# Two transformer blocks on one core: the experts' normalised tokens stored in eight runs of 128 features

## The chip, the cores and the metric

The kernel runs on one core of one Trainium2 chip, in one launch. The metric is the device time of an execution in microseconds; the time of a kernel is the median of its runs.

## What is computed

The program computes two models one after the other on 512 tokens of 1024 features: four layers with convolution, state-space and RWKV mixers, and then two layers (l = 0, 1) of a token mixer and a mixture of experts. The change lies in the mixture of experts alone, of which this is the core (32 experts in four groups of eight, top 2, 512 hidden features; h is the RMS-normalised token, scaled and shifted):

```python
def hierarchical_moe(h, rg_w, rg_b, re_w, re_b, w1, w3, w2):
    xf = h.reshape(N, D)
    g_logits = (xf @ rg_w).astype(jnp.float32) + rg_b
    g_idx = jnp.argmax(g_logits, axis=-1).astype(jnp.int32)
    ...
    top_l, top_i = lax.top_k(e_logits, TOP_K)
    e_w = jax.nn.softmax(top_l, axis=-1) * g_w
    expert_id = (g_idx[:, None] * EXPERTS_PER_GROUP + top_i).reshape(-1).astype(jnp.int32)
    ...
    def run_block(args):
        toks, wts, e = args
        xb = x_pad[toks]
        hb = jax.nn.silu(xb @ w1[e]) * (xb @ w3[e])
        return (hb @ w2[e]) * wts[:, None].astype(xb.dtype)
```

In the layer it stands as `x = x + g2 * hierarchical_moe(rms_norm(x, norm2_g[l]) * (1 + sc2) + sh2, ...)`.

## The kernel before

The residual is held with features on the partitions, as eight tiles `xp[m]` of 128 features by 512 tokens in fp32. `moe(l)` runs once for each of the two layers.

**Normalised tokens.** The loop at L2475 transposes the residual on TensorE (L2479): for each of four blocks j of 128 tokens and each half q of the features, four transposes fill a PSUM tile with 128 tokens by 512 features. ACT multiplies it by the token's 1/rms and writes `hH`, rounded to fp32r, TensorE's format for fp32 operands (L2481). The rest that the rounding leaves is `hL`, so that two fp32r products give an fp32 one: for q = 1 DVE makes it from PSUM (L2483), for q = 0 ACT writes an unrounded copy `xr` (L2486) and POOL subtracts (L2487). Both are tiles of 128 tokens by 4 blocks by 1024 features, in the order of the features. DVE and POOL work at the same time on the routing (`route`), which gives each token its place among its experts' rows.

**Gathers.** `moe_gather` fetches the tokens of a group of places. A group is a run of experts in the order of work; there are seven in a layer, of N = 192, 288, 320, 320, 256, 320 and 64 places. POOL and DVE build a 0/1 selection matrix `R` (L2443, L2444), and TensorE multiplies: each of eight parts j takes 8 matmuls (4 token blocks of hH, then 4 of hL) into one PSUM tile, with 128 features as the stationary operand and `R`, N columns wide, moving. The expert weights lie so that partition p holds the features 8p to 8p+7, so part j needs the features j, j+8, j+16, ...; the stationary operand is `[:, i % 4, j::8]`, one float in eight (L2453). ACT or DVE scale and shift the part into `xg` (L2457, L2455). PSUM tiles of tag "st" have two buffers.

**Experts.** For each expert six tiles `raw` of 1 MB hold its weights (two halves each of w1, w3, w2), loaded on SP's queue (L2383) into 11 buffers. A load is issued when the buffer's last user on TensorE is done. `moe_up` multiplies the gathered tokens with w1 and w3 (L2400), with the tokens stationary and the weights moving; `moe_down` transposes the gated product (L2419) and multiplies with w2 (L2427); `moe_store` copies the result to a block of rows (L2634), and each full block of 128 rows is multiplied by its selection (L2582, L2583) and added to the residual by DVE (L2558).

**Order.** All engines work in the order in which the program issues. The first group is gathered ahead of the first expert, the following ones in pieces: after each expert's `moe_up` the call `self.fill(fill, 5 if g < 1 else 3)` issues some steps of the next group's gather, so that it is ready when its first expert begins. `last_selections` uses the storage of hH and hL again, after the last gather, for the last two blocks' rows. The loop in `overflow` ran no iteration.

Other lines that the rows below name: L423 is the dense layers' matmul, whose stationary operand is 128 adjacent fp32r weights in each partition; L458 is a column sum, a matmul with 128 adjacent fp32 floats as the stationary operand and one moving column. In the first model, L855 is an ACT copy out of PSUM that reads in steps of eight and writes eight runs of 64; L925 is an ACT function of a PSUM tile read in order; L926 is a DVE product that reads an SBUF and a PSUM operand in steps of eight; L994 is a DVE operation that reads PSUM in steps of 64.

Of the kernel before, what the change touches and what calls it, by code (L numbers as in the profile page):

```python
# [8 lines left out]
FT = mybir.dt.float32  # L9
FR = mybir.dt.float32r  # L10
I32 = mybir.dt.int32
AF = mybir.ActivationFunctionType
OP = mybir.AluOpType
# [4 lines left out]
S = 512  # L18
D = 1024
# [1502 lines left out]
class K2(K):  # L1522
# [908 lines left out]
    def moe_gather(self, l, place, base, n, out, N=320, bufs=2):  # L2431

        nc = self.nc
        V, G, T, ACT = nc.vector, nc.gpsimd, nc.tensor, nc.scalar
        s, X = self.tl(f"sh{N}", (2, 4)), f"{N}" if N < 320 else ""
        if isinstance(base, int):
            (V if base else G).tensor_scalar(s, place, float(-base), None, op0=OP.add)
        else:
            V.tensor_scalar(s, place, base, None, op0=OP.subtract)
        R = self.tl("R" + X, (4, N), FR, bufs)  # L2440
        for j in range(4):
            a = self.tl("Ra" + X, (N if X else S,), bufs=bufs)
            G.tensor_scalar(a[:, :n], self.cm("slot")[:, 0:n], s[:, 0, j:j + 1], None, op0=OP.is_equal)  # L2443
            V.scalar_tensor_tensor(R[:, j, :n], self.cm("slot")[:, 0:n], s[:, 1, j:j + 1], a[:, :n],  # L2444
                                   op0=OP.is_equal, op1=OP.add)
        yield
        x = self.tl("xg" + X, (8, N), bufs=bufs)
        out.append(x)
        gain, shift = self.gp[:, l, 0], self.gp[:, l, 1]
        for j in range(8):  # L2450
            p = self.pt("st", bufs=2)
            for i in range(8):
                T.matmul(p[:, :n], (self.hH, self.hL)[i // 4][:, i % 4, j::8], R[:, i % 4, :n], start=i == 0, stop=i == 7)  # L2453
            if j % 2 and out[1:]:
                V.tensor_scalar(x[:, j, :n], p[:, :n], gain[:, j:j + 1], shift[:, j:j + 1], op0=OP.mult, op1=OP.add)  # L2455
            else:
                ACT.activation(x[:, j, :n], p[:, :n], AF.Identity, scale=gain[:, j:j + 1], bias=shift[:, j:j + 1])  # L2457
            yield

    def moe(self, l, begin):  # L2460
        ro = ExitStack()
        self.ro = ro.enter_context(self.tc.tile_pool(name="ro", bufs=1, reuse_waits="tile"))
        nc, A, mo = self.nc, self.A, self.mo
        V, G, T, ACT = nc.vector, nc.gpsimd, nc.tensor, nc.scalar
        loads = {0: self.moe_loads(l, 0), 1: self.moe_loads(l, 1, self.NRAW - 6)}
        if begin:
            self.moe_before(l)
            for k in range(KT):
                self.moe_part(l, k)
        rstd = self.rms_rows(self.ps2, D)  # L2470
        route = self.route(l, rstd)

        self.hH = mo.tile([128, 4, D], FR, name=f"hH{l}", tag="hH", bufs=1)
        self.hL = mo.tile([128, 4, D], FR, name=f"hL{l}", tag="hL", bufs=1)
        for j in range(4):  # L2475
            for q in range(2):
                p = self.pt()
                for k in range(4):
                    T.transpose(p[:, k * 128:k * 128 + 128], self.xp[q * 4 + k][:, j * 128:j * 128 + 128], self.ident)  # L2479
                h, lo = (a[:, j, q * 512:q * 512 + 512] for a in (self.hH, self.hL))  # L2480
                ACT.activation(h, p, AF.Copy, scale=rstd[:, j:j + 1])  # L2481
                if q:
                    V.scalar_tensor_tensor(lo, p, rstd[:, j:j + 1], h.bitcast(FT), op0=OP.mult, op1=OP.subtract)  # L2483
                else:
                    u = self.ro.tile([128, 512], FT, name=f"xr{l}{j}", tag="xr", bufs=2)
                    ACT.activation(u, p, AF.Copy, scale=rstd[:, j:j + 1])  # L2486
                    G.tensor_tensor(lo, u, h.bitcast(FT), OP.subtract)  # L2487
        main = next(route)
        gx = []
        first = self.moe_gather(l, main, *GROUPS[0], gx)  # L2490
        next(first)
        main = next(route)
        self.fill(first, 99)
        wts, over, eii = next(route)
        ro.close()
        with self.tc.tile_pool(name="ov", bufs=1, reuse_waits="tile") as self.ov:
            self.overflow(l, eii, over, wts)
        self.sc = ro.enter_context(self.tc.tile_pool(name="scat", bufs=1, reuse_waits="tile"))
        self.block = -1, None
        prev, fill, g = None, None, -1  # L2500
        for i, r in enumerate(ORDER):
            if r not in loads:
                e = r if r < NSTATIC else nc.values_load(eii[0:1, r:r + 1], engines=[mybir.EngineType.SP], min_val=0, max_val=31)
                loads[r] = self.moe_loads(l, e)
            ws, rest = loads[r]
            self.fill(rest, 6)
            if g < 0 or PLACE[r] >= sum(GROUPS[g]):
                self.fill(fill, 99)
                g += 1
                fill = self.moe_gather(l, main, *GROUPS[g + 1], gx) if g + 1 < len(GROUPS) else None  # L2510
                if not fill:
                    self.last_selections(l, spread)
            o = PLACE[r] - GROUPS[g][0]
            units = [(o + u, min(CAPS[r] - u, 64)) for u in range(0, CAPS[r], 64)]
            gs = self.moe_up(ws, gx[g], units)
            self.fill(fill, 5 if g < 1 else 3)
            if prev:
                self.moe_store(blocks, *prev)
            else:

                spread = []
                for a in (main[:, 0], main[:, 1], wts[:, 0], wts[:, 1]):
                    p = self.pt("tp", bufs=2)
                    self.spread(p, a)
                    self.uid += 1
                    spread.append(self.sc.tile([128, S], FT, name=f"sp{self.uid}", tag=f"sp{len(spread)}"))
                    last = (V.tensor_copy if len(spread) % 2 else ACT.copy)(spread[-1], p).ins
                if self.lb is None:
                    with self.behind(last):
                        self.lower_bounds()  # L2530
                blocks = [self.moe_block(l, b, spread) for b in range(len(BLOCKS))]
            prev = ws, gs, units, r
        self.moe_store(blocks, *prev)
        self.end_block(blocks)
        ro.close()
# [50 lines left out]

    def last_selections(self, l, spread):

        h, lo = (self.mo.tile([128, 4, D], FR, name=f"{n}{l}e", tag=n, bufs=1) for n in ("hH", "hL"))
        self.ends = []  # L2590
        for i, a in enumerate((h, lo)):
            parts = a.rearrange("p a (b n) -> p (a b) n", n=S)
            w = self.tl("sh320", (2, 4))[:, 0]
            self.ends.append([parts, self.selection(len(BLOCKS) - 2 + i, spread, parts[:, 0], w)])

# [263 lines left out]
```

## Time and profile before

| | |
|---|---|
| time, median of 3 runs | 3482.0 us (3480.37 to 3494.45) |
| the profiled execution's own time | 3500.02 us |
| its span, first to last instruction | 3498.2 us |
| mean granted TensorE clock | 0.902 of full speed |
| PE (matmuls) busy | 3143.2 us, 90%, 23218 instructions |
| PEld (weight loads) busy | 2286.1 us, 65%, 23218 instructions |
| DVE busy | 2005.3 us, 57%, 3911 instructions |
| ACT busy | 1031.4 us, 29%, 1695 instructions |
| POOL busy | 875.1 us, 25%, 738 instructions |

PE is TensorE's matmul stream and PEld its loads of stationary operands, which overlap the matmuls. The granted clock is 1.00 for 2.4 GHz and 0.50 for 1.2 GHz; over a stretch a mean of the two is shown. Busy shares are means over the whole program. The two runs of the expert layer lie at about 1968 to 2590 us and from 2890 us to the end. A wait is put down to the engine and line whose end released it. Matmuls follow each other before the one ahead has ended, so the mean duration of one is longer than the interval between two.

### The profile page before, as it was taken

The numbers are of one execution on the slowest core, as the hardware profiler recorded it, in microseconds if no ns is written. First come the engines' busy times: TensorE is split into PE (matmuls) and PEld (weight loads), VectorE is DVE, ScalarE is ACT, GpSimd is POOL, SyncE is SP. The second block draws the span as 40 slices with busy tenths as digits, with TensorE's granted clock in tenths as the row PEclk, the third lists the DMA queues.
The fourth block names the chain that finished last, engine by engine and source line by source line (L and its number), as shares of the span: only waits on it lengthen the run. The fifth ranks groups of instructions, "written<-read, shape, count | busy, mean of one in ns | idle before, by whom it ended". The sixth has DMA issues, their size and how long they took to land. (4 is left out here: it accounts for less than half of the span.)

```text
span 3498.2 us, 57476 instructions
## 1 busy us (share of the span) xinstructions
PE 3143.2 (90%) x23218; PEld 2286.1 (65%) x23218; DVE 2005.3 (57%) x3911; ACT 1031.4 (29%) x1695; POOL 875.1 (25%) x738
## 2 busy tenths in 40 slices
PE   6999889898878889998699889989979997998998
PEld 5687768765657777786565676556647575665564
DVE  6744584566865776888656444424346744344333
ACT  3233334365433333222343321111125332111111
POOL 2911321234223454412124221001011522010000
PEclk9999899998885888998798889999989887999998
DMA  5453552316676545776310349999952004799997
GB/s 167 129 150 104 154 159 79 103 54 172 185 211 175 174 134 157 204 232 165 82 49 9 127 160 381 382 373 405 387 187 67 19 25 181 302 385 379 416 381 293
DMA packets 443070, 690.46 MB, mean 197 GB/s; under 512 B 68720, under 2 KB 354800, under 8 KB 408944
## 3 DMA queue, kind: packets, MB, share of 16 engines
q1 hardware_dynamic: 441648, 684.63, 57.0%
q8 instruction: 185, 3.03, 0.4%
q10 hardware_dynamic: 1152, 2.10, 0.2%
q14 instruction: 85, 0.70, 0.1%
HBM read 642.08 MB, written 46.94 MB: 197 GB/s over the span
## 5 line engine op out<-in xcount | busy, mean ns | idle before, releaser
L317 DVE TENSOR_TENSOR wl<-wr,wh 128x1024 fp32r<-128x1024 f32 (+2 forms) x275 | 324.6, 1182 | 214.9 <-ACT wh L315 104.8
L315 ACT ACTIVATE wh<-wr 128x1024 fp32r<-128x1024 f32 (+2 forms) x290 | 270.7, 939 | 550.7 <-PE pmm L423 184.9
L2400 PE MATMUL pmm<-raw,xg 128*32 128x128 f32 (+1 forms) x5120 | 357.2, 330 | 0.0
L2400 PEld LDWEIGHTS pmm<-raw,xg 128*32 128x32 f32 (+1 forms) x5120 | 231.9, 125 | 118.8 <-issue 50.0
L2543 POOL TENSOR_SCALAR Ra<-sp,cf 128x512 f32<-128x512 f32 x28 | 44.6, 1593 | 883.2 <-PE pst L2582 820.1
L423 PE MATMUL pmm<-H,wh 128*128 128x512 f32 x680 | 209.5, 418 | 9.6 <-ACT cg L2073 4.0
L423 PE MATMUL pmm<-H,wl 128*128 128x512 f32 x680 | 204.3, 409 | 1.3 <-DVE wl L317 1.3
L423 PE MATMUL pmm<-L,wh 128*128 128x512 f32 x680 | 203.4, 408 | 0.1
L2558 DVE SCALAR_TENSOR_TENSOR xp<-pst,mod,xp 128x512 f32<-128x512 f32 x196 | 142.8, 748 | 69.7 <-PE pst L2583 65.0
L2427 PE MATMUL pas<-raw,gT 128*32 128x256 f32 (+1 forms) x1472 | 167.2, 450 | 12.1 <-DVE gT L2421 9.4
L2453 PE MATMUL pst<-R,hH 128*128 128x320 f32 (+4 forms) x448 | 137.7, 429 | 31.7 <-DVE R L2444 29.3
L423 PEld LDWEIGHTS pmm<-H,wh 128*128 128x128 f32 x680 | 131.9, 199 | 42.6 <-ACT cg L2073 4.2
L1556 DVE SCALAR_TENSOR_TENSOR war<-wa,cs,war 128x256 f32<-128x256 f32 x252 | 155.9, 634 | 3.8
L423 PEld LDWEIGHTS pmm<-H,wl 128*128 128x128 f32 x680 | 132.2, 197 | 34.4 <-issue 3.6
L2453 PEld LDWEIGHTS pst<-R,hH 128*128 128x128 f32 x448 | 118.7, 334 | 52.8 <-DVE R L2444 33.1
L423 PEld LDWEIGHTS pmm<-L,wh 128*128 128x128 f32 x680 | 131.8, 196 | 31.1 <-issue 1.7
L2453 PE MATMUL pst<-R,hL 128*128 128x320 f32 (+4 forms) x448 | 127.3, 412 | 0.0
L2634 ACT COPY Y<-pas 32x256 f32<-32x256 f32 (+1 forms) x92 | 37.8, 411 | 296.0 <-DVE Y L2634 295.9
L2634 DVE COPY Y<-pas 32x256 f32<-32x256 f32 (+1 forms) x92 | 43.7, 475 | 133.8 <-PE pas L2427 126.2
L2427 PEld LDWEIGHTS pas<-raw,gT 128*32 128x32 f32 (+1 forms) x1472 | 59.7, 119 | 91.8 <-issue 56.6
L2453 PEld LDWEIGHTS pst<-R,hL 128*128 128x128 f32 x448 | 119.0, 338 | 0.4 <-issue 0.4
L2407 DVE TENSOR_TENSOR g<-g,pmm 128x256 f32<-128x256 f32 (+1 forms) x56 | 20.3, 363 | 171.8 <-ACT g L2406 171.4
(869 smaller groups left out, 6796.1 us busy)
## 6 DMA issues: line engine op xcount, KB each, us to landing
raw<-in_w_dram SPq DMA_DIRECT2D x384, 1024.0 KB, 9.8
wa<-in_w_ada_dram SPq DMA_DIRECT2D x48, 1024.0 KB, 6.3
wr<-in_conv_w_in_dram SPq DMA_DIRECT2D x64, 512.0 KB, 4.8
wr<-in_w_in_dram SPq DMA_DIRECT2D x34, 512.0 KB, 4.1
wr<-in_ple_gate_dram SPq DMA_DIRECT2D x16, 1024.0 KB, 5.4
wr<-in_rwkv_w_rkvz_dram SPq DMA_DIRECT2D x16, 1024.0 KB, 5.3
wr<-in_conv_w_out_dram SPq DMA_DIRECT2D x8, 1024.0 KB, 5.2
wr<-in_ssm_w_in_dram SPq DMA_DIRECT2D x8, 1024.0 KB, 6.4
```

The lines of the kernel that those rows point to most:

```text
L315: self.nc.scalar.activation(h, x, AF.Copy)
L317: (eng or self.nc.vector).tensor_tensor(l, x, h.bitcast(FT), OP.subtract)
L423: nc.tensor.matmul(ps[i], ws[i][w][:, perm[k]], x[k], start=n == first[i], stop=n == last[i])
L1556: E.scalar_tensor_tensor(acc, w[:, k], cs[:, k:k + 1], acc, op0=OP.mult, op1=OP.add)
L2400: nc.tensor.matmul(p[c * n:c * n + n, w // 2 * W:w // 2 * W + W], x[:, j, o:o + n], ws[w][:, jj, c * W:c * W + W], start=j == 0, stop=j == 7)
L2407: nc.vector.tensor_tensor(g, g, p[:, 0:W], OP.mult)
L2427: nc.tensor.matmul(py[q * n:q * n + n, 0:W], gT[:, o:o + n], ws[4 + j // 2][:, j % 2, q * W:q * W + W], start=j == 0, stop=j == 3)
L2453: T.matmul(p[:, :n], (self.hH, self.hL)[i // 4][:, i % 4, j::8], R[:, i % 4, :n], start=i == 0, stop=i == 7)
L2543: G.tensor_scalar(a, P[0], s, None, op0=OP.is_equal)
L2558: self.done = self.nc.vector.scalar_tensor_tensor(self.xp[m], p, self.mod[l][:, 40 + m:41 + m], self.xp[m], op0=OP.mult, op1=OP.add).ins
L2634: (nc.scalar.copy if q % 2 else nc.vector.tensor_copy)(self.block[1][o:o + n, q * W:q * W + W], p[q * n:q * n + n])
```

## The change

hH and hL become tiles of 128 tokens by 4 blocks by 8 runs by 128 features: run j holds the features j, j+8, j+16, ... A gather's stationary operand is then one run, 128 adjacent floats. The reordering is done where the transposed tokens are read from PSUM: the ACT and DVE instructions read PSUM in steps of eight and write eight runs of 64, `xr` is written in that order too, and POOL reads it in order and hH in runs of 64. `last_selections` asks for its two tiles in another shape of the same size.

```diff
@@ moe_gather
             for i in range(8):
-                T.matmul(p[:, :n], (self.hH, self.hL)[i // 4][:, i % 4, j::8], R[:, i % 4, :n], start=i == 0, stop=i == 7)
+                T.matmul(p[:, :n], (self.hH, self.hL)[i // 4][:, i % 4, j], R[:, i % 4, :n], start=i == 0, stop=i == 7)
@@ moe
-        self.hH = mo.tile([128, 4, D], FR, name=f"hH{l}", tag="hH", bufs=1)
-        self.hL = mo.tile([128, 4, D], FR, name=f"hL{l}", tag="hL", bufs=1)
+        self.hH = mo.tile([128, 4, 8, 128], FR, name=f"hH{l}", tag="hH", bufs=1)
+        self.hL = mo.tile([128, 4, 8, 128], FR, name=f"hL{l}", tag="hL", bufs=1)
...
-                h, lo = (a[:, j, q * 512:q * 512 + 512] for a in (self.hH, self.hL))
-                ACT.activation(h, p, AF.Copy, scale=rstd[:, j:j + 1])
+                h, lo = (a[:, j, :, q * 64:q * 64 + 64] for a in (self.hH, self.hL))
+                runs = p.rearrange("t (p j) -> t j p", j=8)
+                ACT.activation(h, runs, AF.Copy, scale=rstd[:, j:j + 1])
                 if q:
-                    V.scalar_tensor_tensor(lo, p, rstd[:, j:j + 1], h.bitcast(FT), op0=OP.mult, op1=OP.subtract)
+                    V.scalar_tensor_tensor(lo, runs, rstd[:, j:j + 1], h.bitcast(FT), op0=OP.mult, op1=OP.subtract)
                 else:
-                    u = self.ro.tile([128, 512], FT, name=f"xr{l}{j}", tag="xr", bufs=2)
-                    ACT.activation(u, p, AF.Copy, scale=rstd[:, j:j + 1])
+                    u = self.ro.tile([128, 8, 64], FT, name=f"xr{l}{j}", tag="xr", bufs=2)
+                    ACT.activation(u, runs, AF.Copy, scale=rstd[:, j:j + 1])
                     G.tensor_tensor(lo, u, h.bitcast(FT), OP.subtract)
@@ last_selections
-        h, lo = (self.mo.tile([128, 4, D], FR, name=f"{n}{l}e", tag=n, bufs=1) for n in ("hH", "hL"))
+        h, lo = (self.mo.tile([128, 8, S], FR, name=f"{n}{l}e", tag=n, bufs=1) for n in ("hH", "hL"))
         self.ends = []
-        for i, a in enumerate((h, lo)):
-            parts = a.rearrange("p a (b n) -> p (a b) n", n=S)
+        for i, parts in enumerate((h, lo)):
```

On every engine's queue the instructions, their order and their waits are the same before and after; only operand shapes of the lines above differ, and line numbers of the code after L2472 are higher by one or two.

## Rows read from the trace of the kernel before

**Rows 1.** Windows of busy time: a piece of one opening, the two loaded stretches.

```profile
core 0: us, PE busy (x) PEld busy (x) DVE busy (x) ACT busy (x) POOL busy (x), PEclk, DMA share, GB/s
2050.00:2100.00 50.00, 50.00 (x558) 39.65 (x546) 18.25 (x51) 12.97 (x23) 6.42 (x5) 1.00 0.56 210
2100.00:2550.00 450.00, 421.04 (x4331) 268.53 (x4331) 187.91 (x378) 58.31 (x124) 36.98 (x29) 0.96 0.98 387
...
3000.00:3450.00 450.00, 420.58 (x4430) 271.99 (x4420) 189.27 (x383) 59.46 (x127) 36.71 (x29) 0.96 0.98 387
```

**Rows 2.** Waits of SP's queue, 2030 to 3490 us: total us, times, longest.

```profile
SPq L2383 <- PE pmm L2400: 308.4, 164, 15.0
```

**Rows 3.** Waits of TensorE's weight loads for weight tiles, same stretch and columns.

```profile
PEld pmm L2400 <- DMA raw<-in_w_dram: 3.1, 7, 0.7
```

**Rows 4.** DMA view, 2100 to 2550 us: forty slices' rate, weight tiles' issues.

```profile
GB/s 349 419 275 385 386 418 417 416 342 415 319 383 422 376 384 418 399 276 370 314 387 417 416 414 418 416 414 414 371 385 410 379 418 308 399 385 417 373 422 415
...
raw<-in_w_dram SPq DMA_DIRECT2D x167, 1024.0 KB, 9.8
```

**Rows 5.** Groups of instructions by shape, 2018 to 3498 us: the hH matmuls.

```profile
L2453 PE MATMUL pst<-R,hH 128*128 128x320 f32 x192 | 60.9, 432 | 5.5 <-DVE R L2444 5.5
...
L2453 PE MATMUL pst<-R,hH 128*128 128x256 f32 x64 | 20.1, 428 | 1.8 <-DVE xg L2455 1.3 <-DVE R L2444 0.5
L2453 PE MATMUL pst<-R,hH 128*128 128x192 f32 x64 | 20.0, 452 | 19.5 <-DVE R L2444 19.4
L2453 PE MATMUL pst<-R,hH 128*128 128x288 f32 x64 | 19.0, 419 | 0.0
...
L2453 PE MATMUL pst<-R,hH 128*128 128x64 f32 x64 | 17.8, 405 | 4.8 <-DVE R L2444 3.9 <-DVE xg L2455 0.9
```

**Rows 6.** Windows of L2453 alone: PE, PEld, granted clock, DMA share, GB/s.

```profile
2021.78:2035.50 13.72, 13.72 (x58) 13.72 (x58) 0.50 0.01 2
2442.00:2446.00 4.00, 3.94 (x16) 3.90 (x16) 0.83 1.01 412
3095.70:3100.78 5.08, 5.08 (x22) 5.08 (x22) 1.00 1.03 427
3368.30:3371.90 3.60, 3.60 (x16) 3.60 (x16) 1.00 1.04 422
3409.00:3417.00 8.00, 5.89 (x24) 5.88 (x24) 0.81 1.01 415
```

**Rows 7.** Windows of L423 alone (columns as in the group before).

```profile
544.84:640.06 95.22, 95.22 (x421) 78.83 (x420) 1.00 0.30 97
1212.52:1219.15 6.63, 6.63 (x58) 6.63 (x57) 1.00 0.77 258
```

**Rows 8.** Windows of L458 alone (columns as in the group before).

```profile
1994.04:1995.01 0.97, 0.96 (x8) 0.97 (x8) 1.00 0.97 405
2591.43:2594.42 2.99, 2.99 (x16) 2.99 (x16) 0.50 0.61 199
```

**Rows 9.** Single lines: min/median/max ns, first and last start, shapes.

```profile
L855 ACT ACTIVATE ut<-pas x4: 597/598/600, 387.9 to 425.8; 128x512 f32<-128x512 f32 x4
...
L925 ACT ACTIVATE zs<-pas x4: 581/598/598, 440.2 to 476.4; 128x512 f32<-128x512 f32 x4
...
L926 DVE TENSOR_TENSOR z<-zs,pas x4: 1058/1088/1172, 447.7 to 491.6; 128x512 f32<-128x512 f32 x4
...
L994 DVE SCALAR_TENSOR_TENSOR xp<-xp,pas x4: 687/688/689, 590.6 to 619.9; 128x512 f32<-128x512 f32 x4
...
L2483 DVE SCALAR_TENSOR_TENSOR hL<-pmm,ry,hH x8: 737/746/752, 2000.3 to 2912.3; 128x512 fp32r<-128x512 f32 x8
...
L2487 POOL TENSOR_TENSOR hL<-xr,hH x8: 1265/1272/1278, 1999.0 to 2911.8; 128x512 fp32r<-128x512 f32 x8
```

**Rows 10.** Timeline: start, duration, and in brackets the idle before it.

```profile
2012.61 0.24 POOL L2284 TENSOR_SCALAR main<-r 128x8 f32<-128x8 f32 x1 [5.64 <-DVE r L2281]
...
2018.42 0.55 PE L2453 MATMUL pst<-R,hH 128*128 128x192 f32 x1 [8.54 <-DVE R L2444]
```

## The prediction

> **What bounds the kernel now.** I read the windows of busy time first. Each of the two expert layers has an opening, in which TensorE is busy without a gap while the DMA engines carry 210 GB/s at a share of 0.56, and a loaded stretch of 450 us and more, in which TensorE is busy for 421 of 450 and the DMA engines show a share of 0.98 at 387 GB/s (of the openings one piece stands in [rows 1]). Two resources are nearly full at once, so next come the waits. SP, which issues the weight tiles, waits for TensorE's last use of a buffer: 164 waits with 308.4 us behind one group of the matmuls of L2400 alone [rows 2]. In the other direction TensorE's weight loads waited for a weight tile 7 times, 3.1 us in all [rows 3]. So the tiles lie ready, TensorE is the late one, and DMA is the resource just behind it. A microsecond taken from TensorE's stream is a microsecond of time until the tiles no longer lie ready.
>
> The gathers are part of that stream. Over both layers there are 64 matmuls with hH at each of N = 192, 288, 256 and 64 moving columns and 192 at N = 320 [rows 5]. As many with hL go beside them, one for one in the code, so there are 128 at each width and 384 at N = 320. Their mean duration of 405 to 452 ns is not the interval at which they follow each other, since they overlap. The interval comes from windows in which nothing but gathers runs: 13.72 us for 57 intervals at N = 192, 5.08 for 21 at N = 320, 3.60 for 15 at N = 64 [rows 6], that is 0.241, 0.242 and 0.240 us. The window of N = 192 is at a granted clock of 0.50 (1.2 GHz), the other two at 1.00 (2.4 GHz). Neither the width nor the clock matters: what all of them share is the stationary operand of 128 columns in steps of eight floats. The weight-load engine is busy for the whole of all three [rows 6].
>
> **What the change takes away.** It makes that operand contiguous. Matmuls with a contiguous stationary operand of 128 x 128 in the same format follow each other after 95.22/420 = 0.227 us at N = 512 and 6.63/57 = 0.116, say 0.117, at N = 256 [rows 7]. With a single moving column, where only the load can set the pace, 8 took 0.97 us at full clock (0.121) and 16 took 2.99 at half clock, 0.187 by plain division, and I take 0.213 (2.99/14, two of the sixteen left to start and end) [rows 8]. So the price after is 0.213 at N = 192 (half clock), 0.117 at N = 256, 0.131 and 0.145 at N = 288 and 320 (on the line between 0.117 and 0.227), and at N = 64 0.121 at full and 0.213 at half clock. For N = 64 I need the share of either clock: six windows hold these gathers, with a mean granted clock of 0.81 (the first and the last of them in [rows 6]); between 0.50 and 1.00 that is 62% at full.
>
> The sum, against 0.241: N = 192, 128 x 0.028 = 3.6 us; N = 288, 128 x 0.110 = 14.1; N = 320, 384 x 0.097 = 37.2; N = 256, 128 x 0.124 = 15.9; N = 64, 128 x (0.62 x 0.120 + 0.38 x 0.028) = 10.9. Together 81.7 us. The first two, 17.7, lie in the openings; the other 64 lie in the two loaded stretches, 32 in each.
>
> **What of it comes out.** The opening's 17.7 us come out whole: the DMA engines are far from their limit there [rows 1]. In a loaded stretch the weights must arrive in 32 us less. By the share there is room for 450 x 0.02 = 9 us. By the rate there is more: the slices at full flow carry about 418 GB/s, others fall to 275 [rows 4], and 387 at 418 leaves 450 x (1 - 387/418) = 33 us. Beside that the stretch begins with tiles loaded ahead: a tile is issued every 450/167 = 2.7 us, so 11 buffers make a round of 30 us, of which 9.8 is the transfer [rows 4] and a few tiles are in use; some 15 us are lead. I take the middle of 9 and 33, 21, and a third of the lead, 26 of the 32. Gain: 17.7 + 2 x 26 = 70 us. The profiled execution took 3500.0 us around its span of 3498.2, 18 over the median of 3482.0; taking 70 from each gives 3430 for such an execution and **3412** by the median.
>
> **What the change adds.** No instruction is added, moved or given another wait; only shapes change. ACT's 24 reads and DVE's 8 now read PSUM in steps of eight and write eight runs of 64. An ACT Copy that does just this is L855: 0.598 us, against 0.598 for a plain PSUM read of that size (L925). DVE's L994 reads PSUM in steps of 64 and takes 0.688, less than L2483 now with 0.746 [rows 9]. So I take nothing for both. The upper bound is L926, which reads both operands in steps of eight: 1.088 [rows 9], 0.342 more, 2.7 us for eight. It would not be hidden: DVE's hL stand between the route's steps, and TensorE idles 8.54 us for the route's first R [rows 10]. POOL's four hL per layer, 1.27 us each [rows 9], read runs of 64 in one operand; behind them POOL idles 5.64 us for DVE [rows 10], which would hide all but a trifle of even a doubling.
>
> A rule speaks against that nothing. The Trainium skill ("Vector Engine (DVE) Microarchitecture Reference", 5.2 Measured stream behaviour on trn2) has DVE streams in SBUF with steps of 24 words at 2.50 ns a column instead of about 1.05. If it held for PSUM in steps of eight, a read of 512 would be an estimated 1.28 us, the eight would cost 4.3 us more, and the forecast would be 3416. The PSUM rows here do not agree with it.
>
> With shorter gathers their evacuation could become the limit: two PSUM buffers, a part of 8 matmuls in 0.94 (N = 256) to 1.16 us (N = 320) instead of 1.93. TensorE now waits for an evacuation 2.2 us in all in these rows (xg) [rows 5]; doubled it is some 2 us, inside the range.
>
> **Rivals.** *DMA is the bound at once* (0.20). Then a loaded stretch gives only the 9 us that the share leaves: 17.7 + 18 = 36, 3446. For it: the share of 0.98. Against: the tiles lie ready [rows 3], and slices of 275 to 350 GB/s stand among those of 418 [rows 4].
>
> *The step is not what makes the load slow* (0.04). If the load has its price by format, or by something else that gathers share, nothing is gained: 3482. Against it: matmuls in the same format at 0.117, and one-column matmuls at 0.121 [rows 7, 8]. The Trainium skill ("TensorE: Matmul & The Clock Gate", LDWEIGHTS) counts the columns alone for a load, some 107 ns for 128, whatever their step; by that the time would stay at 3482. The 0.241 us of the gathers does not agree with it.
>
> *Slower, by the clock* (0.03). Where TensorE comes to wait for tiles in the loaded stretches, its granted clock may fall; the opening's gathers ran at 0.50 after TensorE had idled for R [rows 6, 10]. If the mean of 0.96 [rows 1] fell to 0.87 in both, they would take 2 x (450 x 0.96/0.87 - 450) = 93 us more: 3412 + 93 = 3505. It eats the gain of 70 at about 0.89. Against it: TensorE would still be busy for some nine tenths.
>
> *Faster yet, by the clock* (0.15). Windows with gathers at N = 64 stand at a mean of 0.81 now [rows 6], below the stretch around them; shorter ones would pull less at its mean. If loaded stretches go from 0.96 to 0.98, 2 x 450 x (1 - 0.96/0.98) = 18 us more: 3394.
>
> **The numbers.** My own case holds .58, with 3400 (all 81.7 out) to 3428 around it. The range for 8 in 10 runs from 3384, past the clock's gain, to 3452, past the DMA rival; outside lie .07 for the step that isn't it and the slower case, and some .1 for the far tails of the other two. Less than about 0.5%, 17 us, a measurement of this kernel cannot tell from no change. Faster .92: mine, the DMA rival and the clock's gain, less a tail. Same .05: the step that isn't it, and a DMA case worse than priced. Slower .03: the clock.
>
> **What would show it.** In the profile after, windows of gathers alone should give 0.145 us at N = 320 and 0.12 at N = 64; L2481, L2486 and L2483 should keep their means within 3%; the spans from the first gather to the first loaded stretch should shrink by 9 us per layer; loaded stretches should move over 400 GB/s and TensorE's waits for tiles grow from 3 us to some tens. It would be wrong if gathers stay at 0.24 us, if DVE's reads come near 1.1 us, or if TensorE's waits for tiles take more than half of the 64 us.

## The result and the profile after

| | before | after |
|---|---|---|
| time, median of 4 runs | 3487.85 us (3480.37 to 3494.45) | 3402.94 us (3395.55 to 3410.17) |
| ratio, with its 95% interval | | 0.9754 (0.973 to 0.9779) |
| span of the profiled execution | 3498.2 us | 3393.8 us |
| mean granted TensorE clock | 0.902 | 0.913 |

The change makes the kernel 2.46% faster: of the 3482.0 us of the prediction's time before that is 86 us (77 to 94), against 70 forecast and 81.7 in the full sum. The two profiled spans lie 104.4 us apart, but 9.5 of that lie ahead of the code that the change touches: DVE's first hL already starts at 1990.8 instead of 2000.3 us.

I divided each expert layer at four marks: the first gather, the first matmul of a gather with N = 320, the last gather's last matmul, and the end of the last w2 matmul. That makes an opening, a loaded stretch and a tail. First the windows of before (the columns of the windows in [rows 1]: us, busy us of PE, PEld, DVE, ACT and POOL with their instructions, granted clock, DMA share, GB/s):

```profile
2018.40:2094.70 76.30, 72.72 (x724) 57.20 (x724) 29.01 (x92) 17.45 (x30) 12.79 (x12) 0.82 0.35 126
2094.70:2510.40 415.70, 391.00 (x3968) 252.56 (x3964) 172.06 (x345) 54.89 (x116) 33.42 (x27) 0.97 0.97 385
2510.40:2577.10 66.70, 58.99 (x534) 32.02 (x536) 20.95 (x45) 5.66 (x13) 3.56 (x2) 0.90 0.79 317
2924.50:3003.00 78.50, 72.04 (x723) 57.20 (x723) 28.39 (x79) 12.99 (x24) 13.36 (x12) 0.82 0.34 123
3003.00:3416.30 413.30, 388.67 (x3936) 251.18 (x3932) 171.29 (x344) 54.72 (x116) 33.15 (x27) 0.97 0.98 387
3416.30:3482.70 66.40, 57.70 (x568) 32.30 (x568) 21.52 (x46) 5.83 (x14) 3.56 (x2) 0.94 0.79 320
```

The same windows of the changed kernel:

```profile
2008.90:2073.20 64.30, 58.33 (x723) 43.45 (x723) 28.98 (x92) 17.44 (x30) 12.82 (x12) 0.89 0.42 149
2073.20:2453.00 379.80, 354.65 (x3967) 217.47 (x3964) 171.08 (x344) 54.34 (x116) 33.40 (x27) 0.98 1.01 413
2453.00:2518.40 65.40, 55.46 (x535) 29.92 (x536) 21.52 (x46) 6.34 (x15) 3.56 (x2) 0.97 0.92 373
2864.30:2930.50 66.20, 58.33 (x724) 44.17 (x724) 28.30 (x79) 12.99 (x24) 12.76 (x12) 0.89 0.40 145
2930.50:3309.70 379.20, 353.18 (x3936) 216.16 (x3932) 170.79 (x342) 53.67 (x114) 33.15 (x27) 0.98 1.01 411
3309.70:3378.00 68.30, 56.51 (x567) 30.74 (x568) 21.85 (x49) 7.00 (x15) 3.56 (x2) 0.98 0.89 366
```

The openings went from 76.3 to 64.3 and from 78.5 to 66.2 us, the loaded stretches from 415.7 to 379.8 and from 413.3 to 379.2. That is 12.0 + 12.3 + 35.9 + 34.1 = 94.3 us; the tails moved by no more than 2.0 each. It is more than the 86 of the medians: the profiled execution of before took 12 us more than its median, that of the changed kernel 7 less. In the loaded stretches TensorE's busy time fell by 36.4 and 35.5 us, so nearly all of what TensorE saved came out as time. What the DMA engines had to do for it is in the last two columns: their share went from 0.97 and 0.98 to 1.01, the rate from 385 and 387 to 413 and 411 GB/s. The granted clock rose a little, from 0.97 to 0.98 in the loaded stretches and from 0.82 to 0.89 in the openings.

The gathers' share of it shows in windows of L2453 alone, here the first layer's loaded stretch before and after (PE, PEld, clock, share, GB/s):

```profile
2094.70:2510.40 415.70, 84.54 (x320) 79.16 (x320) 0.97 0.97 385
...
2073.20:2453.00 379.80, 51.62 (x319) 45.00 (x320) 0.98 1.01 413
```

That is 32.9 us of the 36.4; in the second layer it is 84.56 to 52.30, 32.3 of the 35.5. The other 3 us of each are TensorE's other work, of which a clock of 0.98 instead of 0.97 is worth an estimated 3 us (306 x 0.01/0.98).

The gathers, in windows from the start of one run of matmuls to the start of its last, so that n + 1 weight loads make n intervals (PE, PEld, clock, share, GB/s, as in [rows 6]):

```profile
2011.73:2020.24 8.51, 8.51 (x59) 8.51 (x60) 0.77 0.01 3
2061.98:2064.06 2.08, 2.08 (x15) 2.08 (x16) 1.00 0.87 366
2073.23:2075.54 2.31, 2.31 (x16) 2.31 (x16) 1.00 1.02 426
2251.56:2255.44 3.88, 3.88 (x31) 3.83 (x32) 1.00 1.04 423
2412.79:2414.49 1.70, 1.70 (x16) 1.70 (x16) 1.00 1.01 402
2867.10:2876.27 9.17, 9.17 (x59) 9.17 (x60) 0.71 0.00 0
```

N = 320 now takes 2.31/15 = 0.154 us, N = 288 takes 2.08/15 = 0.139, N = 256 3.88/31 = 0.125, and N = 64 1.70/15 = 0.113 at full clock. The first gather, N = 192, takes 8.51/59 = 0.144 at a mean clock of 0.77 in the first layer and 9.17/59 = 0.155 at 0.71 in the second, where the clock stood at 0.50 before [rows 6].

The lines that now read PSUM in steps of eight, and POOL's, against L2483 and L2487 of before [rows 9] (min/median/max ns):

```profile
L2483 ACT ACTIVATE hH<-pas,ry x8: 668/690/696, 1988.1 to 2850.2; 128x512 fp32r<-128x512 f32 x8
...
L2485 DVE SCALAR_TENSOR_TENSOR hL<-pmm,ry,hH x8: 740/746/752, 1990.8 to 2852.1; 128x512 fp32r<-128x512 f32 x8
...
L2489 POOL TENSOR_TENSOR hL<-xr,hH x8: 1262/1268/1272, 1989.5 to 2851.6; 128x512 fp32r<-128x512 f32 x8
```

DVE's median is the same 746 ns and POOL's 1268 stands against 1272: the steps cost nothing.

The waits of SP's queue, 2030 to 3390 us, and of TensorE's weight loads, 2010 to 3390 us (us, times, longest), against [rows 2] and [rows 3]:

```profile
SPq L2383 <- PE pmm L2400: 249.8, 146, 11.5
```

```profile
PEld pmm L2400 <- DMA raw<-in_w_dram: 7.0, 11, 1.0
```

SP waits less for TensorE, 249.8 against 308.4 us, and TensorE waits for tiles 7.0 us at this place where it was 3.1. DMA from 2080 to 2480 us, to be held against [rows 4]:

```profile
GB/s 393 416 363 417 412 418 418 413 423 412 388 422 413 415 422 413 410 417 413 417 416 406 415 419 412 415 417 414 418 418 413 418 416 414 418 417 412 417 414 415
...
raw<-in_w_dram SPq DMA_DIRECT2D x161, 1024.0 KB, 13.7
```

The dips to 275 are gone: all slices but one (363) lie between 388 and 423 GB/s. A tile takes 13.7 us from issue to landing where it took 9.8. That fits transfers that now stand behind each other all the time, though no row shows the queue itself.

### The profile page after: what moved, and what is told of

It is laid out like the page before. It is cut to its first block, busy times and chain, and to the rows that moved or that the text cites. A ratio compares the mean times of both kernels' runs of the same rounds, so it can differ in the third digit from the quotient of the medians.

```text
span 3393.8 us, 57476 instructions
## 1 busy us (share of the span) xinstructions
PE 3023.4 (89%) x23218; PEld 2174.3 (64%) x23218; DVE 2006.5 (59%) x3911; ACT 1031.5 (30%) x1695; POOL 876.2 (26%) x738
## 5 line engine op out<-in xcount | busy, mean ns | idle before, releaser
L2400 PE MATMUL pmm<-raw,xg 128*32 128x128 f32 (+1 forms) x5120 | 348.6, 323 | 5.0 <-DMA raw<-in_w_dram 4.1
L423 PE MATMUL pmm<-H,wh 128*128 128x512 f32 x680 | 206.8, 414 | 9.2 <-ACT cg L2073 4.0
L423 PE MATMUL pmm<-H,wl 128*128 128x512 f32 x680 | 204.3, 408 | 2.0 <-DVE wl L317 2.0
L423 PE MATMUL pmm<-L,wh 128*128 128x512 f32 x680 | 202.4, 406 | 0.1
L423 PEld LDWEIGHTS pmm<-H,wh 128*128 128x128 f32 x680 | 130.6, 197 | 41.7 <-ACT cg L2073 4.2
L423 PEld LDWEIGHTS pmm<-H,wl 128*128 128x128 f32 x680 | 131.5, 196 | 34.8 <-issue 3.6
L423 PEld LDWEIGHTS pmm<-L,wh 128*128 128x128 f32 x680 | 131.1, 195 | 30.6 <-issue 1.7
L2453 PE MATMUL pst<-R,hH 128*128 128x320 f32 (+4 forms) x448 | 91.9, 321 | 33.3 <-DVE R L2444 30.3
L2406 ACT ACTIVATE g<-pmm 128x256 f32<-128x256 f32 (+1 forms) x56 | 18.9, 338 | 301.1 <-PE pmm L2400 301.1
L2400 PE MATMUL pas<-raw,xg 128*32 128x128 f32 (+1 forms) x2048 | 97.3, 292 | 11.7 <-SPq L2505 6.6
L2453 PEld LDWEIGHTS pst<-R,hH 128*128 128x128 f32 x448 | 69.4, 201 | 55.2 <-DVE R L2444 35.5
```

What stands on the lines that cost most here:

```text
L423: nc.tensor.matmul(ps[i], ws[i][w][:, perm[k]], x[k], start=n == first[i], stop=n == last[i])
L2400: nc.tensor.matmul(p[c * n:c * n + n, w // 2 * W:w // 2 * W + W], x[:, j, o:o + n], ws[w][:, jj, c * W:c * W + W], start=j == 0, stop=j == 7)
L2453: T.matmul(p[:, :n], (self.hH, self.hL)[i // 4][:, i % 4, j], R[:, i % 4, :n], start=i == 0, stop=i == 7)
```

## The experiments

Two theories of where the time came from, and two of what bounds the kernel now. **G**: the whole gain is the gathers' interval; storing in runs costs nothing. **S**: the storing side gives or costs something of its own. **D**: in the loaded stretches DMA has become the bound. **P**: TensorE still is.

**Gathers alone, first try.** The kernel before with

```diff
-                T.matmul(p[:, :n], (self.hH, self.hL)[i // 4][:, i % 4, j::8], R[:, i % 4, :n], ...)
+                T.matmul(p[:, :n], (self.hH, self.hL)[i // 4][:, i % 4, j * 128:j * 128 + 128], R[:, i % 4, :n], ...)
```

Expected: 

> The kernel before with one edit: the gathers take 128 adjacent floats of the old storage, so every part holds other features than it should (the experts' inputs are permuted); the PSUM reads stay in order as before. Theory G (the whole gain is the interval of the gathers, 0.241 to 0.118 to 0.147 us, and the stepped PSUM reads cost nothing): the time of the changed kernel, ratio to before 0.9755 within 0.003. Rival S (the storing side costs or gives something of its own): by the dearest DVE row, 0.342 us for each of eight reads, this kernel would be 3 us faster than the changed one; if a part of the gain came from the storing side, say a third, the ratio would be 0.984.

Measured: 3444.88 us, ratio 0.9891 (0.9865 to 0.9916). Neither theory's number, and for a reason that has nothing to do with them: with permuted inputs the second layer's routing came out otherwise and the overflow loop, which runs no turn in the kernels before and after, ran one. Its opening took 113.1 us, while the first layer's opening took 63.8 and its loaded stretch 379.9, as in the changed kernel. The run was made again without that.

**Gathers alone.** The same edit, and the count of overflow turns made zero on the device:

```diff
-        V.tensor_copy(ei[:, 32 + n:], oend[:, 31:32])
+        V.tensor_scalar(ei[:, 32 + n:], oend[:, 31:32], 0.0, None, op0=OP.mult)
```

Expected: 

> The run with adjacent floats out of the old storage again, with the count of overflow turns multiplied by zero on the device (it is zero in the changed kernel too), because the permuted inputs sent the second layer once through the overflow loop, some 45 us in its opening. The first layer of that run, which took no such turn, had an opening of 63.8 and a loaded stretch of 379.9 us, as the changed kernel. Theory G: ratio to before 0.9755 within 0.003. Rival S, a third of the gain from the storing side: 0.984.

Measured: 3403.95 us, ratio 0.9757 (0.9732 to 0.9783). That is the changed kernel's 0.9754. Its openings and loaded stretches, in windows:

```profile
2009.10:2074.90 65.80, 60.36 (x723) 45.92 (x723) 28.94 (x92) 17.44 (x30) 12.78 (x12) 0.88 0.40 146
2074.90:2456.60 381.70, 356.33 (x3968) 217.41 (x3963) 171.12 (x344) 54.27 (x115) 33.41 (x27) 0.98 1.01 410
2870.70:2936.70 66.00, 58.25 (x723) 44.14 (x723) 28.30 (x80) 12.98 (x24) 12.87 (x12) 0.89 0.40 145
2936.70:3315.60 378.90, 353.28 (x3939) 215.58 (x3931) 170.80 (x342) 53.67 (x114) 33.14 (x27) 0.98 1.01 411
```

65.8, 381.7, 66.0 and 378.9 us: within 2 us of the changed kernel, at the same rate. G holds; S would have needed 0.984, or a time some 3 us shorter. Three microseconds are less than the interval can tell, but the windows don't show them, and DVE's duration in the next run speaks against them.

**Storing alone.** The changed kernel with gathers that again take one float in eight:

```diff
-                T.matmul(p[:, :n], (self.hH, self.hL)[i // 4][:, i % 4, j], R[:, i % 4, :n], ...)
+                flat = (self.hH, self.hL)[i // 4].rearrange("t a j n -> t a (j n)")
+                T.matmul(p[:, :n], flat[:, i % 4, j::8], R[:, i % 4, :n], ...)
```

Expected: 

> The changed kernel with one edit: the gathers again take one float in eight, now out of the eight runs, so that the parts hold other features than they should; storing and PSUM reads stay as changed. Theory G: the time of before, ratio 1.000 within 0.003, gathers every 0.241 us. Rival S: with a third of the gain on the storing side 0.992; with stepped reads that cost 3 to 4 us 1.001, to be seen in the duration of DVE's eight hL (0.746 us if they cost nothing, 1.09 to 1.28 if they cost).

Measured: 3482.55 us, ratio 0.9996 (0.9978 to 1.0013). One weight load of a gather, and DVE's hL out of PSUM in steps of eight:

```profile
L2454 PEld LDWEIGHTS pst<-R,hL x448: 312/338/345, 2005.9 to 3401.9; 128*128 128x128 f32 x150
...
L2486 DVE SCALAR_TENSOR_TENSOR hL<-pmm,ry,hH x8: 739/746/751, 1984.3 to 2898.9; 128x512 fp32r<-128x512 f32 x8
```

The load is at 338 ns and DVE's read at 746. With the gathers alone and the storing alone, the four corners fit: the gain goes with the operand's step, and the storing side is worth nothing that can be measured (the interval of the second ends at 8 us of gain and 5 of cost).

**A step for each part.** The changed kernel with the stationary operand of part j taken from the flat tile in a step of its own, each on its own line (steps 1, 2, 3, 4, 5, 6, 8 and 16 at L2455, L2457 and so on to L2469):

```diff
-                T.matmul(p[:, :n], (self.hH, self.hL)[i // 4][:, i % 4, j], R[:, i % 4, :n], ...)
+                flat = (self.hH, self.hL)[i // 4].rearrange("t a j n -> t (a j n)")[:, i % 4 * 1024:]
+                if j == 0:
+                    T.matmul(p[:, :n], flat[:, 0:128:1], R[:, i % 4, :n], ...)
+                if j == 1:
+                    T.matmul(p[:, :n], flat[:, 0:255:2], R[:, i % 4, :n], ...)
...
+                if j == 6:
+                    T.matmul(p[:, :n], flat[:, 0:1017:8], R[:, i % 4, :n], ...)
```

Expected: 

> The changed kernel with a step of its own for the stationary operand of each part j = 0 to 7 of a gather: 1, 2, 3, 4, 5, 6, 8 and 16 floats, each part on its own line; the parts hold other features than they should. Read are the interval of the matmuls in windows at 64 and 256 columns and the mean of one weight load. Theory L (the load pays for each 16-byte stretch of a partition that it touches; the page SBUF - State Buffer of the Trainium skill, section Door 1, says lines of 16 bytes, two hits in one wanted for full rate): 0.112 to 0.118 us at steps 1 and 2, something between at 3, 0.241 from 4 on, the same for 5, 6, 8 and 16. Rival E (any step that isn't 1 is read float by float): 0.241 at 2 and 3 too. Rival B (what counts is that steps of eight fall on the same few memory banks): 3 and 5 cheap, 4, 8 and 16 dear and growing.

Its time of 3494.83 us says nothing (an overflow turn again). What it was for are the loads, here those of hL (min/median/max ns of one):

```profile
L2455 PEld LDWEIGHTS pst<-R,hL x60: 187/188/337, 1998.5 to 3347.9; 128*128 128x128 f32 x60
...
L2457 PEld LDWEIGHTS pst<-R,hL x60: 193/197/331, 1999.6 to 3348.7; 128*128 128x128 f32 x60
...
L2459 PEld LDWEIGHTS pst<-R,hL x60: 261/262/329, 2001.3 to 3365.6; 128*128 128x128 f32 x60
...
L2461 PEld LDWEIGHTS pst<-R,hL x60: 330/330/334, 2003.1 to 3367.3; 128*128 128x128 f32 x60
...
L2463 PEld LDWEIGHTS pst<-R,hL x60: 316/319/325, 2004.9 to 3369.3; 128*128 128x128 f32 x60
...
L2465 PEld LDWEIGHTS pst<-R,hL x60: 316/321/327, 2006.7 to 3406.7; 128*128 128x128 f32 x60
...
L2467 PEld LDWEIGHTS pst<-R,hL x60: 334/337/344, 2008.6 to 3409.8; 128*128 128x128 f32 x60
...
L2469 PEld LDWEIGHTS pst<-R,hL x60: 294/317/320, 2010.4 to 3411.5; 128*128 128x128 f32 x60
```

188 and 197 ns at steps 1 and 2, 262 at 3, 330, 319 and 321 at 4, 5 and 6, 337 at 8 and 317 at 16. The same as intervals, in windows of the lines of steps 2 (N = 288), 3 (N = 64), 4 (N = 288) and 8 (N = 320), each from a part's first matmul to its eighth, seven intervals:

```profile
2029.80:2030.73 0.93, 0.93 (x7) 0.93 (x8) 1.00 1.00 361
...
2424.26:2425.50 1.24, 1.24 (x8) 1.24 (x8) 1.00 1.04 406
...
2034.83:2036.46 1.63, 1.63 (x7) 1.63 (x8) 1.00 0.04 10
...
2106.98:2108.66 1.68, 1.68 (x7) 1.68 (x8) 1.00 1.03 424
```

0.93/7 = 0.133, 1.24/7 = 0.177, 1.63/7 = 0.233 and 1.68/7 = 0.240 us; the first is the pace of N = 288 with adjacent floats and so no load's price at all. This is theory L: a price that follows how many 16-byte stretches are touched, two floats in each almost for nothing (197 against 188 ns), and level from one float in each on. E falls, since step 2 is free; B falls, since 5 and 6 are as dear as 4 and 16 is no dearer than 8. The Trainium skill has such lines for SBUF reads ("SBUF — State Buffer", Door 1: lines of 16 bytes, at least two hits in one for the full rate); steps 1 and 2 and those from 4 on agree. The stride of 4 fp32 that the same paragraph calls free is not borne out: 262 ns at step 3 and 330 at step 4. At step 3, 128 floats touch 96 stretches, three quarters, and 0.177 is three quarters of 0.236. The few per cent between 4, 5, 8 and 16 are left unexplained.

**Half of the gathers' work.** The changed kernel without the hL products:

```diff
-            for i in range(8):
-                T.matmul(..., start=i == 0, stop=i == 7)
+            for i in range(4):
+                T.matmul(..., start=i == 0, stop=i == 3)
```

Expected: 

> The changed kernel without the four hL products of each gather part: 448 matmuls left out, and with them the low half of the gathered tokens. By the intervals of the changed kernel they are 62 us of TensorE, 18 in the openings and 44 in the loaded stretches. Theory P (TensorE still sets the time): all of it comes out, 3403 - 62 = 3341, ratio to before 0.958. Theory D (at 413 GB/s of some 418 DMA has become the bound of the loaded stretches): the 18 of the openings and about 5 per stretch come out, 3375, ratio 0.968, and TensorE's waits for weight tiles grow to some 30 us.

Measured: 3380.5 us, ratio 0.9701 (0.9672 to 0.9729): by the two ratios 18 us less than the changed kernel, where 58 us of gathers are gone (windows of L2453). D's 0.968 lies in the interval, P's 0.958 far outside. Loaded stretch and tail of each layer:

```profile
2061.90:2433.60 371.70, 338.39 (x3807) 196.72 (x3804) 170.17 (x342) 53.12 (x114) 33.17 (x27) 0.96 1.02 416
2433.60:2505.80 72.20, 56.84 (x537) 30.03 (x536) 22.18 (x50) 7.30 (x16) 3.56 (x2) 0.95 0.90 368
...
2918.00:3290.70 372.70, 338.21 (x3810) 194.52 (x3804) 170.47 (x342) 53.53 (x114) 33.41 (x27) 0.97 1.02 416
3290.70:3363.00 72.30, 58.96 (x537) 30.90 (x536) 21.98 (x49) 7.00 (x15) 3.56 (x2) 0.91 0.88 362
```

371.7 + 72.2 = 443.9 and 372.7 + 72.3 = 445.0, where the changed kernel has 445.2 and 447.5. TensorE is busy for 16 and 15 us less in the loaded stretches and the DMA rate there is 416 GB/s, but the sum hardly moves: by rate and time some 181 MB pass in a layer's loaded stretch and tail, here as in the changed kernel. The openings, 60.4 and 60.1 us against 64.3 and 66.2, gave 10 us and not D's 18; their clock was 0.83 instead of 0.89. And the waits of TensorE's weight loads for tiles of w1 and w3 grew from 7.0 us to

```profile
PEld pmm L2400 <- DMA raw<-in_w_dram: 18.1, 19, 1.7
```

**More of the gathers' work.** The changed kernel with the hL products taken twice:

```diff
-            for i in range(8):
-                T.matmul(p[:, :n], (self.hH, self.hL)[i // 4][:, i % 4, j], ..., stop=i == 7)
+            for i in range(12):
+                T.matmul(p[:, :n], (self.hH, self.hL, self.hL)[i // 4][:, i % 4, j], ..., stop=i == 11)
```

Expected: 

> The changed kernel with the four hL products of each gather part taken twice: 448 matmuls added, so that the gathered tokens hold the low half twice. TensorE gets 62 us more, 18 in the openings and 44 in the loaded stretches. Theory P: 3403 + 62 = 3465, ratio to before 0.9935. Theory D: half of the 44 hides behind transfers, 3443, ratio 0.987.

Measured: 3464.41 us, ratio 0.995 (0.9928 to 0.9973). Here P's number came out, 0.9935, not D's 0.987. The loaded stretches:

```profile
2071.90:2487.30 415.40, 390.23 (x4128) 243.59 (x4123) 173.04 (x346) 55.13 (x116) 33.15 (x27) 0.96 0.97 384
2970.80:3385.70 414.90, 390.36 (x4131) 243.18 (x4123) 173.59 (x346) 55.11 (x116) 33.14 (x27) 0.96 0.96 385
```

TensorE is busy 390 of 415 us, and DMA is back at 385 GB/s: within two microseconds these are the loaded stretches of before. They are 35.6 and 35.7 us longer than the changed kernel's, and TensorE's busy time is 35.6 and 37.2 us longer. The gathers alone (windows of L2453: 78.92 and 77.10 us against 51.62 and 52.30) are 27.3 and 24.8 of that, where 22 were forecast; the rest, 8 and 12, is TensorE's other work, of which the clock of 0.96 instead of 0.98 is worth an estimated 6 (303 x 0.02/0.98); the last few stay open. So D as it was priced is wrong on this side. The changed kernel stands at the edge: what is taken from TensorE's gathers now brings little, what is added costs in full.

**Fewer buffers.** The changed kernel with

```diff
-    NRAW, OVER = 11, 16
+    NRAW, OVER = 9, 16
```

Expected: 

> The changed kernel with 9 buffers for weight tiles instead of 11. In the openings all buffers lie full and DMA stands idle. Theory D (DMA sets the pace of the loaded stretches): each buffer less is 1.05 MB more to be moved there at 414 GB/s, 2.5 us, so two of them in two layers cost 10 us, ratio to before 0.978, or more where a shorter round leaves transfers unstarted. Theory P (TensorE sets the pace): nothing, 0.9755.

Measured: 3420.58 us, ratio 0.981 (0.9787 to 0.9832): 18 us over the changed kernel's 3403 by the medians, 20 by the ratios, D's direction with about twice its size. Loaded stretch and tail:

```profile
2070.90:2458.30 387.40, 358.01 (x3967) 219.89 (x3964) 170.87 (x344) 53.83 (x115) 33.20 (x27) 0.96 1.00 407
2458.30:2525.80 67.50, 56.50 (x535) 30.73 (x536) 21.44 (x46) 6.73 (x15) 6.09 (x6) 0.95 1.01 400
2951.20:3339.10 387.90, 355.61 (x3968) 218.03 (x3964) 171.17 (x344) 54.37 (x116) 33.20 (x27) 0.98 1.00 408
3339.10:3405.50 66.40, 56.15 (x535) 29.99 (x536) 21.44 (x46) 6.28 (x14) 3.57 (x2) 0.95 0.92 375
```

454.9 and 454.3 us against 445.2 and 447.5, so 8 us a layer where the two tiles not loaded ahead are 5. DMA's share is 1.00, its rate 407 and 408 instead of 413 and 411. That fits a shorter round that leaves some transfers unstarted, beside the tiles no longer loaded ahead; the two were not told apart. Nor is all of it DMA: in the loaded stretches TensorE's busy time is 3.4 and 2.4 us longer than in the changed kernel.

**TensorE kept busy ahead of the first gather.**

```diff
-        cnt = cs[:, 3]
+        cnt, self.cs = cs[:, 3], cs
...
         main = next(route)
+        p = self.pt("tp", bufs=2)
+        for _ in range(5):
+            T.matmul(p, self.cs.rearrange("t j n -> t (j n)"), self.hH[:, 0, 0:4].rearrange("t j n -> t (j n)").bitcast(FT), start=True, stop=True)
         gx = []
```

Expected: 

> The changed kernel with five fp32 matmuls of 512 columns, their result unused, behind the route's own ones, in the 8.5 us in which TensorE waits for the first selection matrix. Theory C (the opening gained more than the sum because the granted clock came up within the first gather; at 2.4 GHz its matmuls take 0.112 instead of 0.213 us): the first gather stands at 1.00 from its start, which gives about 5 us per layer, 3393, ratio to before 0.9727. Rival: the clock doesn't come up earlier, or the time goes into the wait for the next selection matrix; then 0.9755, and more if the added matmuls delay the gather.

Measured: 3407.08 us, ratio 0.9777 (0.9753 to 0.9802): no gain. The windows of the first layer, from the clock's rise on:

```profile
1997.00:2003.80 6.80, 3.52 (x10) 1.40 (x9) 5.90 (x13) 0.00 (x0) 5.46 (x7) 1.00 0.51 203
2003.80:2010.60 6.80, 6.73 (x32) 6.76 (x32) 6.70 (x31) 1.96 (x4) 3.34 (x3) 0.50 0.00 1
```

The clock did come up ahead of the gather and went down again at 2003.8; in the 6.8 us before that TensorE was busy for 3.5 and waited for R in the rest. 6.8 us at half clock followed, with half of the gather in them. The experiment moved the slow piece and didn't remove it, so it settles nothing on what a first gather wholly at 2.4 GHz would bring.

## Why the prediction was right, and where its sum was off

**The mechanism** was right: the step of the stationary operand set the gathers' interval, and nothing else of the change counts. The two halves of the change, each alone, show it (0.9757 and 0.9996), and the loads by step show why.

**The intervals** were right where the work was at full clock. Priced were 0.145, 0.131, 0.117 and 0.121 us at N = 320, 288, 256 and 64; measured as means of whole runs are 0.154, 0.139, 0.125 and 0.113. Each of these means holds one to three hand-overs from one PSUM tile to the next. The median over all gather matmuls of the trace at full clock, by their starts, is 0.147, 0.133, 0.118 and 0.112, so the price of a matmul itself was right within 0.01 everywhere. At half clock 0.213 was priced and 0.211 measured (the last rows of this document).

**The first gather** was priced too dear. The sum took 0.213 us for all 128 matmuls of N = 192, at half clock as before. The clock came up within the gather, so the mean was 0.144 and 0.155 us in the two layers, and the openings gave 24.3 us instead of 17.7. Why it came up within this gather and not within the same one before no run shows: TensorE is busy throughout in both (8.51 of 8.51 us, 13.72 of 13.72 [rows 6]). That was part of what the rival of a faster clock had in mind, at a place where it didn't look for it.

**"26 of the 32"** is the step that failed in size, and it was the largest choice of the working. It left 6 us in each loaded stretch to the DMA engines. The gathers gave back the 32 that were priced (32.9 and 32.3), and 35.9 and 34.1 came out; the 3 us above the 32 fit TensorE's other work at a clock that rose from 0.97 to 0.98. Both terms of the 26 were too small. Rate times window estimates what a loaded stretch moved: 160.0 MB before and 156.9 after in the first layer, 159.9 and 155.9 in the second; the 3 or 4 MB of difference moved on into the tails (21.1 to 24.4 MB, 21.2 to 25.0). At the rates after, the tiles that moved on are 8 and 10 us where the forecast took 5 of lead, and the higher rate is the other 28 and 24 where it took 21. The share of 0.98 misled: it left 9 us of room, while the rate left 33, and the rate was the nearer one. It went to 413 and 411 GB/s against the 418 taken for full flow. One sign that the forecast named didn't come with it: TensorE's waits for tiles reached 7.0 us and not some tens.

**The DMA rival** was wrong for this change and right for the next one: with another 58 us of gathers taken from TensorE, 18 came out. **The stretch's lead** fits the tiles that moved on into the tails and the run with 9 buffers, where two tiles less cost more than that run's forecast; no run shows it apart from a shorter round.

**No cost of the PSUM reads** was right: 746 ns for DVE before, after and in the storing alone. The rule of the Trainium skill ("Vector Engine (DVE) Microarchitecture Reference", 5.2) that spoke against it was measured there on SBUF; the estimated 1.28 us that it would give for such a read isn't borne out for PSUM in steps of eight. **The rival that the step isn't it** fell with the storing alone and the loads by step; so did, for steps of three and more, the rule of the Trainium skill ("TensorE: Matmul & The Clock Gate", LDWEIGHTS) that a load's price goes by its columns alone. **The slower rival** didn't come: the granted clock rose.

## What to carry to other kernels

Look at how the stationary operand lies within a partition: at 128 columns of four-byte floats a load was cheapest at a step of one or two floats (four or two taken of every 16 bytes; 188 and 197 ns). At full clock and N = 64 the interval was half as long again at a step of three (0.177 against 0.113 us) and twice as long from a step of four on, and at a step of eight no moving width up to 320 hid that. Do the reordering where an engine reads PSUM anyway: there it cost nothing here. And when two resources are both nearly full, read the room of the second from its rate against its best slices rather than from its busy share, and add what may move on past the stretch; here that came closer, and the gain stopped there, as the run with half of the gathers' work shows.

## What the runs showed of the hardware

A load of adjacent floats follows TensorE's clock. The first gather of the changed kernel (N = 192) in two windows, at 1.2 and at 2.4 GHz (PE, PEld, clock, share, GB/s):

```profile
2011.70:2015.70 4.00, 3.97 (x19) 4.00 (x20) 0.51 0.03 6
2015.90:2020.30 4.40, 4.40 (x42) 4.40 (x40) 1.00 0.00 0
```

4.00/19 = 0.211 us against 4.40/39 = 0.113. A load in steps of eight took 0.240 to 0.242 at either clock [rows 6], so it isn't TensorE's clock that paces it. In the run with a step for each part all 60 loads of hL at step 4 took 330 to 334 ns, those of the first gather at 1.2 GHz among them, where those of step 1 went from 187 to 337.

Reading PSUM in steps of eight and writing runs of 64 took ACT and DVE no longer than reading and writing in order: ACT 690 ns before and after, DVE 746. Nor did reading runs of 64 take POOL longer, 1272 and 1268.

16 DMA engines sustained 413 GB/s over 380 us into one core, with a tile's time from issue to landing up from 9.8 to 13.7 us; at that point the busy share reads 1.01, and at 0.97 and 0.98 there were still 7 and 6% of rate left in it.
